# A planner's look-ahead limit for the MLP's second sweep, and the centering of two inner norms on ScalarE, in a one-layer decoder kernel

## The chip, the cores and the metric

The kernel runs on one core of a Trainium2 chip. The metric is device microseconds (us) of one execution; lower is better. A core has five engines that run their own instruction queues in order and wait for each other by semaphores: TensorE (PE in the profile; its weight loads are PEld), VectorE (DVE), ScalarE (ACT), GpSimd (POOL) and SyncE (SP, which here only issues DMAs).

## What is computed

One post-normalised decoder layer over 512 tokens of 1024 features, in float32: every sub-layer does h <- LayerNorm(ALPHA * h + f(h)).

```
h = layer_norm(x, ln_in_g, ln_in_b)
h = layer_norm(ALPHA * h + hybrid_mixer(h, ...), ln_mix_g, ln_mix_b)   # three groups of heads, then h @ w_out
h = layer_norm(ALPHA * h + mem_attn(h, mem, ...), ln_mem_g, ln_mem_b)  # 4 heads over 256 memory tokens
u = relu(h @ w_up + b_up)                                              # 1024 -> 4096
h = layer_norm(ALPHA * h + (u * u) @ w_down + b_down, ln_ffn_g, ln_ffn_b)
```

The norms after the mixer and after the memory attention are called the two inner norms here ("mix" and "mem" in the names). Centering is the step (x - mean) * rs, rs being 1 / sqrt(variance + eps).

## The kernel before, in words

**Precision.** Matrix products are made in the fp32r type, with each operand split in two parts: hi = round(x), lo = x - hi, and three products hi*hi, hi*lo, lo*hi. So for every tile of weights or activations that enters a product there is a cast (hi) and a subtraction (lo). `two_parts` puts the cast on ScalarE and lets VectorE or GpSimd subtract; `split` lets the planner choose the engine of both.

**The planner.** The kernel's code does not issue instructions. It records operations in program order, each with an order number (`prio`, the value of `nc.clock`, which goes up by one with each operation), and at the end `nc.issue(LOOK)` places them one by one: of all operations whose inputs are placed it takes the one that can start first by its own table of prices, and of two with the same start the one with the lower number. The queue of every engine is the order of this placing. The front is the oldest operation that is not placed yet. An operation may be placed before its turn if its number lies at most `min(LOOK, op.ahead)` beyond the front's (line 300; LOOK is 560, `nc.ahead` is 1e9 except in one other stage), and if the buffers that it takes leave enough for all that comes before it in program order (`slots`, line 275).

**Buffers.** `pages` has 31 buffers of 128 x 1024 floats; the residual rows `res` (4), the transposed activations `h2T` (8), the kept MLP rows `keep` (16), and the split rows `a` (two for each step) are all pages. Raw weights (`wr`) have 4 buffers, split weights (`wh`, `wl`) 5 each. A buffer's new user waits for the last reader of the old one.

**The inner norms.** `gemm_tok` makes the 512 x 1024 output of `w_out` (or `w_mem_o`) in four tiles of 128 tokens, one after the other at its end. `after_mix` and `after_mem` are called for each tile: `residual` adds the two PSUM banks to `res[t]`, takes `bn_stats` and `bn_aggr` (mean, variance), `ve` = variance + eps on VectorE and `rs` = ve ** -0.5 on GpSimd; `center` then writes the centered rows in place (VectorE `tensor_scalar`). After every second tile `ln_transposed` transposes the rows on TensorE (`ps_lt`), applies gain and shift (`h`) and splits them into `h1T` or `h2T`, which the next stage's products (`ps_q`, `ps_up`) read. The products of the first 256 tokens can run while tiles 2 and 3 are still being normed.

**The MLP.** 4096 hidden features in 16 steps of 256. The first sweep does for step i two `up` products (`ps_up`, 24 matmuls each), keeps relu(.)^2 in `keep[i]`, and two steps later `first_products(i - 2)`: sums and differences of row blocks and weight blocks, split in `ends`, `mid`, `h_dn`, `l_dn`, and 18 matmuls into six PSUM banks (`ps_dn`; a scheme with 7 products for 8). `first_products(13)`, `(14)` and `(15)` come after the last `up`. The weight sums that the second sweep needs go to DRAM (tile `t`) and come back as `r_t`. The second sweep does the four products that are left: `second_parts(i)` splits `keep[i]` into two pages `a` and loads and splits `r_t` and `r_dn` (8 operations), and 24 matmuls follow, so that one step takes 32 order numbers. The last TAIL = 4 steps have their `second_parts` called together as `rest`, take pages `b` for their weights, and are multiplied tile by tile, so that the final norm overlaps them.

Of the kernel before, what the change touches and what calls it, by code (L numbers as in the profile page):

```python
# [12 lines left out]
AF = mybir.ActivationFunctionType  # L13
OP = mybir.AluOpType
# [350 lines left out]
def trunk_kernel(ctx: ExitStack, tc: tile.TileContext, x, mem, ln_in_g, ln_in_b, w_in, gate_w2,  # L365
# [23 lines left out]
    nc = Program(real)  # L389
    slack = [0.0]  # L390

    def page(shape, dtype, name):
        return pages.tile([128] + shape, dtype, name)
# [7 lines left out]
    def bank(name, shape=(512,)):  # L401
        return psum.tile([128] + list(shape), F32, name)
# [115 lines left out]
    def center(y, mv, rs):  # L518
        nc.vector.tensor_scalar(y, y, mv[:, 0:1], rs, op0=OP.subtract, op1=OP.mult)
# [174 lines left out]
    for j in range(1, NT):  # L694
# [3 lines left out]
        for h in range(IDX_H):  # L698
# [7 lines left out]
            else:  # L706
                nc.vector.scalar_tensor_tensor(acc[:, :n], r[:, :n], iw[:, j, h:h + 1], acc[:, :n],
                                               op0=OP.mult, op1=OP.add)
# [406 lines left out]
    def residual(res, t, parts, name):  # L1115

        n = 512 if len(parts) == 2 else 256
        st = small.tile([128, D // n, 6], F32, "st_" + name)
        for cc, o in parts:
            nc.vector.tensor_tensor(res[t][:, cc], o, res[t][:, cc], op=OP.add)  # L1120
            for c0 in range(cc.start, cc.stop, n):
                nc.vector.bn_stats(st[:, c0 // n, :], res[t][:, c0:c0 + n])
        return mean_scale(st, name)

    def normed(res, t, parts, name):

        mv, rs = residual(res, t, parts, name)
        center(res[t], mv, rs)

    def gain_shift(hat, gb, t, later=0.0):  # L1130
        nc.clock += later
# [6 lines left out]
    res = []  # L1138
# [8 lines left out]
    def after_mix(t, parts):  # L1147
        normed(res, t, parts, "mix")
        if t % 2:
            ln_transposed(res, *gb_cols["mix"], h1T, t - 1, 2)  # L1150
# [47 lines left out]
    def after_mem(t, parts):  # L1198
        normed(res, t, parts, "mem")
        if t % 2:  # L1200
            ln_transposed(res, *gb_cols["mem"], h2T, t - 1, 2)
# [30 lines left out]
    def two_parts(hi, lo, src):  # L1232
        nc.scalar.copy(hi, src)
        any_tt(lo, src, f32(hi), OP.subtract)

    def raw_down(i, k):
        r = wr_pool.tile([128, 1024], F32, f"r_dn{k}")
        nc.sync.dma_start(r, w_down[256 * i + 128 * k:256 * i + 128 * k + 128, :])
        return r
# [5 lines left out]
    def products(banks, todo, p, start, stop):  # L1245

        tt = slice(128 * p, 128 * p + 128)
        for name, (ah, al), (bh, bl) in todo:
            mm3(banks[name, p], ah[:, tt], al[:, tt], bh, bl, start, stop)
# [69 lines left out]
    def second_parts(i, tail):  # L1319

        a = [page([4, 256], F32R, f"a{n}") for n in range(2)]
        two_parts(a[0], a[1], keep[i])
        r0 = wr_pool.tile([128, 1024], F32, "r_t13")
        nc.sync.dma_start(r0, sums[i])
        r1 = raw_down(i, 1)
        right = []
        for r in (r0, r1):
            if tail:
                hi, lo = (page([1024], F32R, f"b{n}") for n in range(2))
            else:  # L1330
                hi, lo = wh_pool.tile([128, 1024], F32R, "h_dn"), wl_pool.tile([128, 1024], F32R, "l_dn")
            two_parts(hi, lo, r)
            right += [(hi[:, L], lo[:, L]), (hi[:, R], lo[:, R])]
        left = [(a[0][:, n, :], a[1][:, n, :]) for n in range(4)]
        return [("7", left[0], right[1]), ("5", left[1], right[0]), ("3", left[3], right[3]), ("2", left[2], right[2])]

    for i in range(NP - TAIL):
        todo = second_parts(i, False)
        if i == 0:
            for name, *_ in todo:  # L1340
                for p in range(2):
                    banks[name, p] = bank(f"ps_dn{name}")
        for one in todo:
            for p in range(2):
                products(banks, [one], p, i == 0, False)
    rest = [second_parts(i, True) for i in range(NP - TAIL, NP)]

# [12 lines left out]
    for p in range(2):  # L1360
        for n, name in enumerate(("7", "5", "3", "2")):
            for i, todo in enumerate(rest):
                products(banks, [todo[n]], p, False, i == TAIL - 1)
            if name == "7":
# [27 lines left out]
M_SLACK = 600.0  # L1392
DOWN_LATER = 60.0
TAIL = 4

_INS = ["x", "mem", "ln_in_g", "ln_in_b", "w_in", "gla_gate_w2", "gla_gate_b", "gla_norm_g", "dsa_w_uv",
        "w_out", "ln_mix_g", "ln_mix_b", "w_mem_q", "w_mem_kv", "w_mem_o", "ln_mem_g", "ln_mem_b",
# [19 lines left out]
```

## Time and profile before

| | |
|---|---|
| three runs of the kernel | 821.04, 821.12, 822.54 us; median 821.12 us |
| the execution that was profiled | 822.55 us, of which 820.8 us are the span from the first instruction to the last |
| busy share of the span | PE 96%, PEld 81%, DVE 78%, ACT 40%, POOL 18% |
| granted TensorE clock, mean | 0.99 |

The rows below come from the trace of that one execution. Times are us from the span's start, durations us, "mean" ns. `[4.17 <-PE ps_up L356]` behind an instruction says that its engine sat idle for 4.17 us ahead of it and which instruction ended that. Every recorded operation has line 356, the planner's issuing line, so rows are told apart by the names of their tiles.

### The profile page before, as it was taken

Reading aid. Unit: us, or ns where it says so; the run is one execution under the profiler, and the core shown is the slowest. Engines: PE = TensorE matmul, PEld = TensorE weight load, DVE = VectorE, ACT = ScalarE, POOL = GpSimd, SP = SyncE. Lnnn points to the kernel's source line nnn. Section 1 sums busy time; section 2 is a strip of 40 time slices with the busy share of each in tenths; the row PEclk is TensorE's granted clock in tenths of the full one; section 3 lists DMA queues with packets and bytes.
Section 4 is the critical chain, followed back from the end, with each engine's and each line's share of the span. In section 5 each row is a group of like instructions: output and inputs, shape, how many; then the busy total and the mean of one; then the engine's idle time right before and its main releaser. Section 6 shows DMA issues by size and latency. Waiting matters only on the chain.

```text
span 820.8 us, 11293 instructions
## 1 busy us (share of the span) xinstructions
PE 790.4 (96%) x4177; PEld 662.5 (81%) x4177; DVE 636.3 (78%) x1118; ACT 328.0 (40%) x631; POOL 144.5 (18%) x169
## 2 busy tenths in 40 slices
PE   7999999999999999999999989999999999899995
PEld 5998768777877888899788888888888888678884
DVE  7737999997649984776953778997777776798778
ACT  5506634577535540244340233223323332585430
POOL 5320141354622210120530120000000000110001
PEclk8999999999999999999999999999999999999998
DMA  8520331603244535041322025466546555467632
GB/s 232 145 54 15 100 94 27 180 9 102 70 139 162 159 139 155 27 127 54 129 77 78 26 78 164 133 216 201 184 148 211 202 167 170 147 214 243 195 126 103
DMA packets 99927, 106.70 MB, mean 130 GB/s; under 512 B 10448, under 2 KB 79136, under 8 KB 99872
## 3 DMA queue, kind: packets, MB, share of 16 engines
q1 hardware_dynamic: 97344, 99.00, 38.5%
q10 hardware_dynamic: 2528, 6.98, 2.5%
q8 instruction: 33, 0.54, 0.3%
q14 instruction: 22, 0.18, 0.1%
HBM read 94.69 MB, written 10.49 MB: 128 GB/s over the span
## 4 chain that ended last, share of the span: by engine, by line
PE 69%; DVE 16%; issue 3%; ACT 1%; POOL 1%; DVEq 0%; ACTq 0%; POOLq 0%
PE ps_up L356 21%; PE ps_dn L356 18%; PE ps_wo L356 5%; PE ps_wmo L356 4%; PE ps_q L356 4%; DVE acc L356 2%; DVE m L356 2%; PE ps_km L356 2%; DVE res L356 2%; PE ps_z L356 2%; PE ps_vm L356 2%; PE ps_dq L356 1%; DVE s L356 1%; PE ps_mo L356 1%; PE ps_ms L356 1%
## 5 line engine op out<-in xcount | busy, mean ns | idle before, releaser
L356 PE MATMUL ps_up<-h2T,h_up 128*128 128x512 f32 (+1 forms) x576 | 163.1, 368 | 0.4 <-POOL h2T L356 0.4
L356 PEld LDWEIGHTS ps_up<-h2T,h_up 128*128 128x128 f32 x576 | 105.4, 191 | 18.2 <-POOL h2T L356 0.6
L356 PE MATMUL ps_up<-h2T,l_up 128*128 128x512 f32 (+1 forms) x288 | 105.9, 368 | 0.0
L356 ACT ACTIVATE ur<-ps_up,gb_all 128x512 f32<-128x512 f32 x32 | 22.1, 690 | 103.6 <-PE ps_up L356 103.4
L356 PEld LDWEIGHTS ps_up<-h2T,l_up 128*128 128x128 f32 x288 | 55.0, 191 | 8.6
L356 PE MATMUL ps_dn<-h_dn,a 128*128 128x512 f32 x192 | 59.2, 389 | 0.0
L356 DVE TENSOR_TENSOR l_dn<-r_dn,h_dn 128x1024 fp32r<-128x1024 f32 (+1 forms) x44 | 45.2, 1027 | 4.9 <-ACT h_dn L356 3.5
L356 PE MATMUL ps_dn<-h_dn,ends 128*128 128x512 f32 x128 | 47.0, 390 | 0.7 <-DVE ends L356 0.7
L356 POOL TENSOR_TENSOR a<-keep,a 128x1024 fp32r<-128x1024 f32 x1 | 4.9, 4924 | 229.9 <-DVE l_dn L356 229.9
L356 PE MATMUL ps_q<-h1T,h_wmq 128*128 128x256 f32 (+1 forms) x192 | 44.7, 323 | 0.3 <-POOL h1T L356 0.3
L356 PEld LDWEIGHTS ps_dn<-h_dn,a 128*128 128x128 f32 x192 | 36.0, 188 | 7.4
L356 ACT ACTIVATE h<-ps_lt,gb_all 128x256 f32<-128x256 f32 x18 | 9.1, 566 | 80.3 <-PE ps_lt L356 80.3
L356 PE MATMUL ps_wmo<-h_wmo,oT 128*128 128x512 f32 x128 | 40.8, 393 | 0.0
L356 PE MATMUL ps_wo<-h_wo,mix 128*128 128x512 f32 x128 | 40.3, 392 | 0.0
L356 DVE TENSOR_TENSOR l_up<-r_up,h_up 128x1024 fp32r<-128x1024 f32 x31 | 37.8, 1223 | 1.9 <-ACT h_up L356 0.5
L356 PE MATMUL ps_dn<-l_dn,a 128*128 128x512 f32 x96 | 37.3, 389 | 0.0
L356 PEld LDWEIGHTS ps_q<-h1T,h_wmq 128*128 128x128 f32 x192 | 32.0, 190 | 2.8 <-POOL h1T L356 0.6
L356 DVE TENSOR_SCALAR h_up<-r_up 128x1024 fp32r<-128x1024 f32 x19 | 13.1, 692 | 22.7 <-PE ps_up L356 16.4
L356 PE MATMUL ps_q<-h1T,l_wmq 128*128 128x256 f32 (+1 forms) x96 | 30.7, 320 | 0.0
L356 PEld LDWEIGHTS ps_dn<-h_dn,ends 128*128 128x128 f32 x128 | 24.0, 188 | 6.1 <-DVE ends L356 1.2
L356 PEld LDWEIGHTS ps_wo<-h_wo,mix 128*128 128x128 f32 x128 | 24.0, 188 | 4.9
L356 PEld LDWEIGHTS ps_wmo<-h_wmo,oT 128*128 128x128 f32 x128 | 24.0, 188 | 4.8
(407 smaller groups left out, 2085.2 us busy)
## 6 DMA issues: line engine op xcount, KB each, us to landing
r_dn<-in_w_down_dram SPq DMA_DIRECT2D x48, 512.0 KB, 4.3
r_up<-in_w_up_dram SPq DMA_DIRECT2D x32, 512.0 KB, 4.2
r_t<-t SPq DMA_DIRECT2D x16, 512.0 KB, 4.1
r_kvv<-in_w_mem_kv_dram SPq DMA_DIRECT2D x8, 512.0 KB, 4.3
r_kvk<-in_w_mem_kv_dram SPq DMA_DIRECT2D x8, 512.0 KB, 3.6
r_wo<-in_w_out_dram SPq DMA_DIRECT2D x8, 512.0 KB, 4.6
r_wmq<-in_w_mem_q_dram SPq DMA_DIRECT2D x8, 512.0 KB, 5.2
r_wmo<-in_w_mem_o_dram SPq DMA_DIRECT2D x8, 512.0 KB, 3.2
```

The lines of the kernel that those rows point to most:

```text
L356: f(*[real(a) for a in args], **{k: real(a) for k, a in kwargs.items()})
```

## The change

Two edits. The centering of the two inner norms is done by ScalarE: VectorE makes a one-column tile off = -mean * rs, and ScalarE computes rs * x + off over the 1024 columns, in place. And the operations of `second_parts` for the first twelve steps of the second sweep get a look-ahead limit of 120 order numbers in place of 560; their products and the four steps of `rest` keep 560.

```
     def normed(res, t, parts, name):

         mv, rs = residual(res, t, parts, name)
-        center(res[t], mv, rs)
+        off = tiny(1, "off_" + name)
+        nc.vector.tensor_scalar(off, mv[:, 0:1], rs, -1.0, op0=OP.mult, op1=OP.mult)
+        nc.scalar.activation(res[t], res[t], AF.Identity, bias=off, scale=rs)
...
     for i in range(NP - TAIL):
+        nc.ahead = SECOND_AHEAD
         todo = second_parts(i, False)
+        nc.ahead = 1e9
...
+SECOND_AHEAD = 120.0
```

Since the planner places all operations together, both edits can change the order of any queue after them.

## Rows read from the trace of the kernel before

**Rows 1.** The page: span, and busy time of each engine with its share.

```profile
span 820.8 us, 11293 instructions
PE 790.4 (96%) x4177; PEld 662.5 (81%) x4177; DVE 636.3 (78%) x1118; ACT 328.0 (40%) x631; POOL 144.5 (18%) x169
```

**Rows 2.** The chain that ended last, in the MLP's first sweep (start, us, what).

```profile
515.99 10.88 PE ps_up L356 x48
526.87 4.08 PE ps_dn L356 x18
```

**Rows 3.** Windows: PE, PEld, DVE, ACT, POOL busy (count), clock, DMA share, GB/s.

```profile
476.20:479.50 3.30, 3.30 (x18) 3.30 (x17) 3.07 (x4) 0.00 (x0) 1.49 (x1) 0.50 0.66 189
...
706.20:724.40 18.20, 13.53 (x56) 9.92 (x55) 18.17 (x31) 9.80 (x16) 5.06 (x2) 1.00 0.59 193
724.40:789.40 65.00, 65.00 (x288) 53.87 (x287) 53.82 (x51) 38.98 (x39) 1.17 (x1) 1.00 0.70 225
```

**Rows 4.** Timeline where the memory attention passes into the MLP (start, us, engine).

```profile
469.95 2.94 ACT L356 CAST h_up<-r_up 128x1024 fp32r<-128x1024 f32 x3 [2.62 <-PE ps_wmo L356]
...
471.58 2.37 POOL L356 TENSOR_TENSOR l_up<-r_up,h_up 128x1024 fp32r<-128x1024 f32 x1
471.65 2.85 DVE L356 TENSOR_SCALAR res<-res,mv_mem,rs_mem 128x1024 f32<-128x1024 f32 x1 [0.67 <-POOL rs_mem L356]
471.75 0.40 PE L356 MATMUL ps_up<-h2T,h_up 128*128 128x256 f32 x2
...
474.64 0.63 PE L356 MATMUL ps_lt<-ident,res 128*128 128x128 f32 x4 [2.03 <-DVE res L356]
...
482.11 1.47 PE L356 MATMUL ps_lt<-ident,res 128*128 128x128 f32 x12
```

**Rows 5.** Timeline where the mixer passes into the memory attention: PE, then DVE.

```profile
350.20 0.40 PE L356 MATMUL ps_q<-h1T,h_wmq 128*128 128x256 f32 x2
...
357.38 1.47 PE L356 MATMUL ps_lt<-ident,res 128*128 128x128 f32 x12
...
360.03 0.62 PE L356 MATMUL ps_q<-h1T,h_wmq 128*128 128x256 f32 x3 [0.35 <-POOL h1T L356]
...
350.20 0.81 DVE L356 TENSOR_SCALAR res<-res,mv_mix,rs_mix 128x1024 f32<-128x1024 f32 x1 [0.67 <-POOL rs_mix L356]
```

**Rows 6.** Groups by shape (busy, mean ns), then tiles (min/median/max ns).

```profile
L356 ACT CAST h_up<-r_up 128x1024 fp32r<-128x1024 f32 x13 | 13.5, 1055 | 21.9 <-PE ps_dn L356 19.3 <-PE ps_wmo L356 2.6
L356 ACT ACTIVATE h<-ps_lt,gb_all 128x256 f32<-128x256 f32 x18 | 9.1, 566 | 80.3 <-PE ps_lt L356 80.3
L356 ACT CAST h2T<-h 128x256 fp32r<-128x256 f32 x10 | 3.5, 417 | 0.0
...
L356 DVE TENSOR_SCALAR res<-res,mv_mem,rs_mem x4: 807/814/2849, 456.3 to 478.5; 128x1024 f32<-128x1024 f32 x4
L356 DVE TENSOR_SCALAR ve_mem<-mv_mem x4: 136/154/154, 455.4 to 476.1; 128x1 f32<-128x1 f32 x4
```

**Rows 7.** Timeline, opening of the kernel: POOL and DVE.

```profile
8.07 1.44 POOL L356 TENSOR_TENSOR rs_in<-ve_in,mhalf 128x1 f32<-128x1 f32 x2 [2.87 <-DVE ve_in L356]
...
8.21 0.16 DVE L356 TENSOR_SCALAR ve_in<-mv_in 128x1 f32<-128x1 f32 x1
```

**Rows 8.** Timeline between the MLP's two sweeps: DVE, POOL, PE.

```profile
701.66 1.23 DVE L356 TENSOR_TENSOR a<-keep,a 128x1024 fp32r<-128x1024 f32 x1 [4.17 <-PE ps_up L356]
...
717.28 2.51 DVE L356 TENSOR_TENSOR keep<-keep,s 128x256 f32<-128x256 f32 x1
...
714.58 4.92 POOL L356 TENSOR_TENSOR a<-keep,a 128x1024 fp32r<-128x1024 f32 x1 [229.87 <-DVE l_dn L356]
...
720.98 0.50 PE L356 MATMUL ps_dn<-l_dn,mid 128*128 128x512 f32 x1 [1.65 <-DVE l_dn L356]
```

**Rows 9.** Tiles `a` and `keep` (min/median/max ns, first and last start us).

```profile
L356 ACT CAST a<-keep x16: 1042/1050/1062, 637.5 to 746.1; 128x1024 fp32r<-128x1024 f32 x16
...
L356 DVE TENSOR_TENSOR keep<-keep,s x16: 416/421/2507, 495.3 to 717.3; 128x256 f32<-128x256 f32 x16
```

## The prediction

> **What bounds the kernel now.** I read the page first: TensorE is busy for 96% of the span, VectorE for 78%, ScalarE for 40% [rows 1]. So an edit can gain only where TensorE stands still or is slowed. The chain of waits shows how regular the rest is: in the MLP's first sweep it consists of runs of 48 `ps_up` and 18 `ps_dn` matmuls without a gap [rows 2], at 10.88 / 48 = 0.227 us for a matmul. Nothing can be won there. The windows, stage by stage, then show two places near the change where TensorE loses time.
>
> The first is the passage from the memory attention to the MLP. The timeline shows TensorE waiting 2.03 us, up to 474.64, for the centered rows of the third tile; their centering on VectorE took 2.85 us while GpSimd ran a `l_up` subtraction of 2.37 us [rows 4], against a median of 0.81 us [rows 6]. After this wait the granted clock is 0.50, which is 1.2 GHz, for 3.30 us [rows 3]: another 1.65 us lost, 3.7 us in all. The passage from the mixer to the memory attention has the same work without the stall: there the centering took 0.81 us, and from TensorE's first product to the twelve transposes of the last tile pass 357.38 - 350.20 = 7.2 us [rows 5], against 482.11 - 471.75 = 10.4 us here [rows 4]. The difference, 3.2 us, is the better price of the stall, since it is what the twin does not pay.
>
> The second is the junction of the sweeps, 706.20 to 724.40. TensorE does the products of `first_products(13)`, `(14)` and `(15)` there, 54 matmuls, which at 0.227 us take 12.2 us; the window lasts 18.2 us, so 6.0 us are lost. VectorE is busy for 18.17 of the 18.2 us [rows 3], so it is the bound. Yet it had idled 4.17 us right before, up to 701.66, at the head of its queue an `a` subtraction of the second sweep that waited for `up` matmuls [rows 8]. By the code the two share no data; what `a` waits for there is a page, one that the last `up` products still read as `h2T`. Behind it on VectorE's queue stood the weight sums of `first_products(14)`. Later GpSimd runs another `a` subtraction for 4.92 us [rows 8], and a `keep` subtraction of VectorE that takes 0.42 us in the median takes 2.51 us beside it [rows 8, 9].
>
> **The change part by part: the limit.** Order numbers from the code: if `second_parts(0)` begins at S, then `first_products(13)` begins at S - 130, `up(31)` at S - 159, `up(30)` at S - 188. With 560 ahead, the first `a` was allowed from about S - 560, some four and a half first-sweep steps (96 numbers each) before `first_products(13)`: at 15 us a step, 10.88 + 4.08 [rows 2], that is about 639 us, and the first cast stands at 637.5 [rows 9]. With 120 it is allowed ten operations into `first_products(13)`, which the front cannot pass before the end of `up(31)` at 706.2. So `a(0)` can no longer stand in VectorE's queue at 701.66. What leaves VectorE's queue ahead of the late matmul at 720.98 is then the wait of 4.17, the subtraction of 1.23, and 2.51 - 0.42 = 2.09 beside GpSimd: 7.5 us, more than the 6.0 us that can be won. Against this: the rows of `rest` keep the old limit. `second_parts(12)` begins at S + 384 and is allowed 560 before that, at S - 176, twelve operations into `up(30)`, or about 697 us. Its rows can fill the same hole. They find two free pages (31, less 8 `h2T`, 4 `res`, 16 `keep` and one `ends`), so they need not wait for `h2T`, but two subtractions, 2.5 us, come back: 5.0 us. And `first_products(15)` needs relu, square and its own chain of small operations after `up(31)`; I take 1 us off for it. **Junction: -4.0 us**, with 0 (the hole stays) and -6.0 as ends.
>
> In the second sweep TensorE is full, 65.00 of 65.00 us, VectorE has 53.82 and ScalarE 38.98 [rows 3]. The limit moves casts from before 746 to later; ScalarE's idle 40% hides them. 120 numbers are 3.75 steps of 24 matmuls, some 20 us, and the loads were held to two steps before by the four `wr` buffers, so SP's queue is hardly changed. Cost: 0; without that cover see the fourth rival.
>
> **The centering.** Removed from VectorE: 8 operations of 0.81. Added: 8 `off`, like `ve` one column, 0.15, and on ScalarE 8 passes over 1024 columns. Such a pass isn't in the trace; a cast of that size takes 1.055, and a 256-column pass with scale and bias from tiles 0.566 against 0.417 for a plain cast [rows 6], so 1.055 + 0.15 = 1.20 us. Bounds: 1.055, and 1.055 + 4 x 0.15 = 1.65 if the extra grew with the columns; I take 1.20, the nearest difference as it stands. With under 0.1 for one hand-over more (the whole detour over GpSimd for `rs` is a wait of 0.67 [rows 5]) the chain of a tile grows by 0.15 + 0.1 + 0.39 = 0.64 us, and VectorE gets 0.66 us back.
>
> Tiles 0 and 1 at both passages are hidden: two more tiles of 24 matmuls, 48 x 0.227 = 10.9 us, follow on TensorE. For tiles 2 and 3 the cover is the next stage's product over the first 256 tokens, and at the mixer's end it just runs out: TensorE waits 0.35 us for `h1T` [rows 5]. There the longer chain shows, less what VectorE gives back: 0 to +0.64, **mixer passage: +0.3 us**. At the MLP's passage the stall goes, because ScalarE's centering stands neither behind GpSimd nor in front of VectorE's next tile; but ScalarE has three casts of `h_up` from 469.95 to 472.89 [rows 4]. The centering is ready at 471.65 + 0.25 = 471.9, as the third cast begins. If it comes behind, it ends at 474.1 and the wait shrinks by 0.4 only, unless the planner has given TensorE products to do before the transposes, which it does when it knows of the delay. Ends: -0.4 and -3.7. I take the twin's 3.2 less 0.6 for the longer chain: **MLP passage: -2.6 us**.
>
> [...]
>
> **Sum.** -4.0 + 0.3 - 2.6 = -6.3 us. Against the profiled execution that is 822.55 - 6.3 = 816.25 (span 814.5 and the same 1.75 around it); that execution is 1.43 above the median of the three, and against the median, which I forecast, it is 821.12 - 6.3 = 814.8 us.
>
> **The rivals.** 1. Only the junction pays: the centering queues behind the third cast, -0.4 + 0.3 - 4.0, 817.0 us. For it: the cast starts within 0.1 us of the centering. Against it: both passages are planned anew.
> 2. `off` is held by GpSimd: it ends at 474.1, the centering at 475.4, TensorE waits 2.9 instead of 2.03; 821.12 - 4.0 + 0.3 + 0.9 = 818.3. Against it: a one-column `tensor_scalar` ran in its usual 0.16 us from 8.21, inside GpSimd's `rs_in` that began at 8.07 [rows 7]. For it: that GpSimd operation has one column too. [...]
> 3. The limit doesn't do what it says, since `rest` is free of it: its rows take the pages and the hole, and the junction loses 6.0 us still. 821.12 + 0.3 - 2.6 = 818.8.
> 4. The second sweep starves, and it gets slower. `rest` may take the 7 pages that are free at its start (31, less 4 `res`, 2 gains, 16 `keep`, 2 `a`) while steps 4 to 11 may not. Then `a` of the next step gets its page only as the last is released, and TensorE waits for a cast of 1.05 and a subtraction of 1.23 in every step: 2.3 us. It is slower than before from (6.3 + 1.6) / 2.3, four such steps; with six of them 821.12 - 6.3 + 13.8 = 828.6. For it: the code's limits. Against it: of two operations that can start together the planner takes the earlier number, and pages get free with every step.
> 5. Neither place pays and nothing is lost, because other orders bring other stalls: 821.1.
>
> **How the numbers follow.** A measurement of this kernel tells about 0.2%, 1.6 us, from no change. Chances: forecast 0.44 (own range 811.4 to 817, from the ends -6.0 and -3.7 to about half the gain), rival 1 0.15, rival 2 0.05, rival 3 0.12, rival 5 0.13, rival 4 0.11. Faster: 0.44 + 0.15 + 0.05 + 0.12 = 0.76; same 0.13; slower 0.11. The range runs from 811.4 (both stalls gone whole) to 821.0, which leaves out rival 4, half of rival 5 and little below.
>
> **What would show it.** Right: no wait of TensorE on centered rows near 472, clock 1.00 in the 12 us after, the twelve transposes some 8 us behind the first `ps_up`; VectorE without an idle stretch between 697 and 702, no `a` on GpSimd, and about 14 us between the last `ps_up` and the first second-sweep matmul; the second sweep still at 0.227 us. Centerings of 1.2 us on ScalarE. Wrong: transposes waiting for ScalarE, `a` of steps 12 and up ahead of `first_products(14)` on a page of `h2T`, or waits on `a` within the second sweep.

## The result and the profile after

The kernel after takes 812.34 us (median of 4 runs, 812.27 to 812.93), the kernel before, run beside it, 821.63 us (821.04 to 822.54). The ratio is 0.9888, 95% interval 0.9874 to 0.9903: 9.3 us or 1.1% faster. Forecast were 814.8 us and a gain of 6.3 us. The direction and the two places were right; both were sized too small, and the mixer passage, where a small loss was forecast, gained a little.

The first lines of the page of the profiled execution after (812.93 us), which answer to [rows 1]: span, and busy time of each engine with its share and count.

```profile
span 811.2 us, 11285 instructions
...
PE 788.2 (97%) x4177; PEld 661.9 (82%) x4177; DVE 630.8 (78%) x1127; ACT 335.1 (41%) x635; POOL 140.2 (17%) x164
```

TensorE did the same 4177 matmuls in nearly the same busy time; the span is 9.6 us shorter. To see where, I took the start of the first or last matmul of each stage from the tiles' rows of both traces; each number is the time from one such start to the next.

| from ... to | before | after |
|---|---|---|
| start ... first `ps_wo` (opening, mixer) | 304.8 | 305.5 |
| ... first `ps_q` (mixer's output) | 45.4 | 45.4 |
| ... first `ps_wmo` (mixer passage, memory attention) | 72.5 | 72.1 |
| ... first `ps_up` (memory's output) | 49.0 | 49.0 |
| ... first `ps_dn` (MLP passage) | 40.0 | 36.0 |
| ... last `ps_up` (first sweep) | 194.3 | 194.3 |
| ... first `ps_dn` on an `a` (junction) | 18.4 | 12.5 |
| ... last `ps_dn` (second sweep) | 86.8 | 86.8 |
| ... end | 9.6 | 9.6 |

The MLP passage gave 4.0 us, the junction 5.9, the mixer passage 0.4. The opening is 0.7 longer. No operation of the change lies in it, and in the profiled executions below the first `ps_wo` starts anywhere from 304.4 to 305.4 us (305.4 in `a0_on_pool`, too, which has neither edit), so I take this for spread.

The windows after (us; PE, PEld, DVE, ACT, POOL busy with counts, clock, DMA share, GB/s), answering to [rows 3]: MLP passage, last `up` products, junction, second sweep.

```profile
472.20:508.20 36.00, 35.90 (x257) 33.80 (x257) 31.08 (x57) 17.37 (x28) 2.51 (x3) 1.00 0.42 134
691.80:702.68 10.88, 10.88 (x50) 9.01 (x49) 9.39 (x14) 4.76 (x7) 0.00 (x0) 1.00 0.43 147
702.68:715.00 12.32, 12.32 (x57) 10.18 (x56) 12.29 (x21) 10.83 (x15) 3.02 (x1) 1.00 0.72 234
715.00:780.00 65.00, 65.00 (x288) 53.85 (x287) 53.52 (x50) 39.98 (x40) 2.42 (x2) 1.00 0.69 223
```

TensorE is busy 35.90 of 36.00 us in the passage, at full clock (1.00, which is 2.4 GHz), and 12.32 of 12.32 in the junction, which is about what 54 matmuls at 0.227 us need (12.3): TensorE has next to no wait left at either place. VectorE is still full in the junction (12.29 of 12.32), but TensorE no longer waits for it.

The timeline after at the MLP passage (start, us, engine, instruction, idle time before it and what ended it), answering to [rows 4].

```profile
472.84 1.06 POOL L356 TENSOR_SCALAR h_up<-r_up 128x1024 fp32r<-128x1024 f32 x1
472.90 0.21 DVE L356 TENSOR_SCALAR off_mem<-mv_mem,rs_mem 128x1 f32<-128x1 f32 x1
...
473.15 1.24 ACT L356 ACTIVATE res<-res,off_mem,rs_mem 128x1024 f32<-128x1024 f32 x1 [5.14 <-DVE off_mem L356]
...
474.06 0.68 DVE L356 TENSOR_SCALAR h_up<-r_up 128x1024 fp32r<-128x1024 f32 x1
474.23 0.93 POOL L356 TENSOR_TENSOR rs_mem<-ve_mem,mhalf 128x1 f32<-128x1 f32 x1 [0.33 <-DVE ve_mem L356]
474.30 1.03 ACT L356 CAST h_up<-r_up 128x1024 fp32r<-128x1024 f32 x1
474.53 0.60 PE L356 MATMUL ps_lt<-ident,res 128*128 128x128 f32 x4
...
476.04 1.25 ACT L356 ACTIVATE res<-res,off_mem,rs_mem 128x1024 f32<-128x1024 f32 x1 [0.71 <-DVE off_mem L356]
477.47 1.47 PE L356 MATMUL ps_lt<-ident,res 128*128 128x128 f32 x12
```

The transposes of the third and fourth tile stand without a wait; the third tile's centering ends at 474.39, 0.14 us before TensorE comes to it. The three `h_up` casts that stood together on ScalarE are spread: GpSimd has one, VectorE one, ScalarE one, between the two centerings.

The timeline after at the junction, answering to [rows 8].

```profile
693.82 0.69 DVE L356 TENSOR_TENSOR r_dn<-r_dn 128x512 f32<-128x512 f32 x1
...
697.05 0.69 DVE L356 TENSOR_SCALAR h_dn<-r_dn 128x1024 fp32r<-128x1024 f32 x1 [1.09 <-PE ps_up L356]
697.85 1.23 DVE L356 TENSOR_TENSOR l_dn<-r_dn,h_dn 128x1024 fp32r<-128x1024 f32 x1
...
700.25 1.22 DVE L356 TENSOR_TENSOR a<-keep,a 128x1024 fp32r<-128x1024 f32 x1
...
702.05 1.22 DVE L356 TENSOR_TENSOR a<-keep,a 128x1024 fp32r<-128x1024 f32 x1
```

The weight sums `r_dn` of `first_products(14)` begin at 693.82, 8.9 us before the last `up` product ends at 702.68. Before, they stood behind the waiting `a` of [rows 8] and began at 702.81, 3.4 us before 706.20:

```profile
702.81 0.69 DVE L356 TENSOR_TENSOR r_dn<-r_dn 128x512 f32<-128x512 f32 x1
```

So they come 5.5 us earlier, measured from the end of the `up` products: the wait of 4.17 and the subtraction of 1.23 [rows 8]. The two `a` rows that do come early, at 700.25 and 702.05, stand behind `l_dn`. They belong to `rest`: with the limit on `rest` too they are gone (`rest_limited` below).

Tiles after (min/median/max ns, first and last start): the new operations, and `a` ([rows 6, 9]).

```profile
L356 DVE TENSOR_SCALAR off_mem<-mv_mem,rs_mem x4: 205/213/215, 456.6 to 475.8; 128x1 f32<-128x1 f32 x4
L356 ACT ACTIVATE res<-res,off_mem,rs_mem x4: 1244/1245/1248, 456.8 to 476.0; 128x1024 f32<-128x1024 f32 x4
...
L356 ACT CAST a<-keep x16: 1037/1048/1054, 699.0 to 751.3; 128x1024 fp32r<-128x1024 f32 x16
L356 DVE TENSOR_TENSOR a<-keep,a x15: 1211/1217/1219, 700.2 to 758.0; 128x1024 fp32r<-128x1024 f32 x15
L356 POOL TENSOR_TENSOR a<-keep,a x1: 2419/2419/2419, 715.0 to 715.0; 128x1024 fp32r<-128x1024 f32 x1
```

### The profile page after: what moved, and what is told of

It is laid out like the page before. It is cut to its first block, busy times and chain, and to the rows that moved or that the text cites. A ratio compares the mean times of both kernels' runs of the same rounds, so it can differ in the third digit from the quotient of the medians.

```text
span 811.2 us, 11285 instructions
## 1 busy us (share of the span) xinstructions
PE 788.2 (97%) x4177; PEld 661.9 (82%) x4177; DVE 630.8 (78%) x1127; ACT 335.1 (41%) x635; POOL 140.2 (17%) x164
## 4 chain that ended last, share of the span: by engine, by line
PE 76%; DVE 10%; issue 2%; ACT 1%; POOL 0%; DVEq 0%; ACTq 0%; POOLq 0%
PE ps_up L356 22%; PE ps_dn L356 19%; PE ps_wmo L356 5%; PE ps_wo L356 5%; PE ps_q L356 4%; PE ps_z L356 2%; PE ps_km L356 2%; PE ps_vm L356 2%; PE ps_gg L356 1%; DVE res L356 1%; PE ps_dq L356 1%; DVE acc L356 1%; PE ps_mo L356 1%; DVE s L356 1%; PE ps_o L356 1%
## 5 line engine op out<-in xcount | busy, mean ns | idle before, releaser
L356 PE MATMUL ps_up<-h2T,h_up 128*128 128x512 f32 (+1 forms) x576 | 161.3, 366 | 0.1
L356 POOL TENSOR_TENSOR l_dn<-r_dn,h_dn 128x1024 fp32r<-128x1024 f32 x1 | 3.1, 3071 | 236.8 <-ACT h_dn L356 236.8
L356 DVE MAX8 m<-acc 128x8 f32<-128x256 f32 (+2 forms) x48 | 25.9, 550 | 0.3
```

Of the source, the lines that this page charges most:

```text
L356: f(*[real(a) for a in args], **{k: real(a) for k, a in kwargs.items()})
```

## The experiments

Medians of the kernel before beside them were 821.41 us (first four), 821.13 us (second four) and 821.46 us (last four). The ratios and their 95% intervals are to those runs; they are taken over all runs, so they are not exactly the quotients of the medians. "Stage" lengths are those of the table above.

### Each half alone: `limit_only` and `centre_only`

The two halves of the diff, each by itself:

```
-        center(res[t], mv, rs)                             # centre_only
+        off = tiny(1, "off_" + name)
+        nc.vector.tensor_scalar(off, mv[:, 0:1], rs, -1.0, op0=OP.mult, op1=OP.mult)
+        nc.scalar.activation(res[t], res[t], AF.Identity, bias=off, scale=rs)
...
+        nc.ahead = SECOND_AHEAD                            # limit_only
         todo = second_parts(i, False)
+        nc.ahead = 1e9
```

> The limit without the ScalarE centering. Theory (the two stalls are separate, and the limit undoes only the one between the sweeps): 6.0 us below the kernel before, about 815.6 us; first ps_dn of the second sweep some 6 us earlier behind the last ps_up, the 2.03 us wait on centered rows and the half clock after it still there. Rival (the gain comes from the new order as a whole, each edit needs the other): less than 4 us.

Measured: 816.15 us, ratio 0.9934 (0.9917 to 0.9950). Junction 12.5 us as after, MLP passage 40.0 as before: a gain of 5.3, near the 5.9 of the junction. The rest went in the second sweep, 87.7 in place of 86.8. The timeline has there one wait of TensorE for an `a`:

```profile
731.27 1.20 PE L356 MATMUL ps_dn<-h_dn,a 128*128 128x512 f32 x4 [0.57 <-DVE a L356]
```

It is not the fourth rival, which has `a` waiting for a page: VectorE was busy for all of the 6 us from 726 to 732 and had other subtractions ahead of this `a` in its queue.

> The ScalarE centering without the limit. Theory: the passage from the memory attention to the MLP gives 4.1 us, the passage from the mixer nothing, the junction stays at 18.2 us: about 817.5 us. Rival (the centering pays at both inner norms, since it frees VectorE): more than 5 us, or, if the longer chain is paid at the mixer's passage, 3 us or less.

Measured: 818.37 us, ratio 0.9964 (0.9951 to 0.9977). The MLP passage is 36.0, the junction 20.0. The waits of TensorE at the junction add up to 4.7 us, as before; the extra 1.6 us are the clock, as the windows of this execution show (same columns as above; 0.75 and 0.59 are means over windows that hold stretches at 1.2 and at 2.4 GHz).

```profile
716.00:719.60 3.60, 3.40 (x11) 2.64 (x12) 3.60 (x7) 2.48 (x3) 0.11 (x1) 0.75 0.58 166
719.60:721.60 2.00, 2.00 (x7) 1.56 (x6) 0.59 (x2) 1.45 (x3) 1.17 (x1) 0.59 0.55 217
```

The two halves gain 5.3 + 3.0 = 8.3 us alone and about 9.2 together, and each is shown to work at its own place.

### What the limit acts on: `rows_limited`, `loads_limited`, `step0_free`, `ahead240`

All four have the new centering. `rows_limited` and `loads_limited` split the limit within `second_parts`:

```
     a = [page([4, 256], F32R, f"a{n}") for n in range(2)]
+    nc.ahead = 1e9 if tail else SECOND_AHEAD      # rows_limited: around this call alone
     two_parts(a[0], a[1], keep[i])
+    nc.ahead = 1e9                                # loads_limited: limit from here to the return
     r0 = wr_pool.tile([128, 1024], F32, "r_t13")
```

In both, the two lines of the change around the call of `second_parts` are taken out.

> The changed kernel with the limit on the rows alone (cast and subtraction of a), the loads and splits of r_t and r_dn free to come 560 ahead. Theory (an early row on a page is what blocks VectorE): as the changed kernel, 812.3 us. Rival (early weights fill the raw-weight buffers and hold up first_products(15)): between 814 and 818.3 us.

> The opposite: the changed kernel with the limit on the loads and splits of r_t and r_dn alone, the rows a free. Theory (rows): the 4.2 us hole of VectorE ahead of first_products(14) and the 6.0 us between the sweeps are back, 818.3 us. Rival (weights): 812.3 us.

Measured: `rows_limited` 812.19 us, 0.9887 (0.9873 to 0.9902), junction 12.5; `loads_limited` 817.92 us, 0.9960 (0.9945 to 0.9974), junction 18.4 with the same four waits of TensorE as before (0.75, 1.87, 0.39 and 1.64 us). The limit works through the rows alone.

`step0_free` lets one step out of it:

```
-        nc.ahead = SECOND_AHEAD
+        nc.ahead = SECOND_AHEAD if i > 0 else 1e9
```

> The kernel after, but the limit leaves out the first step of the second sweep, whose rows may then be taken as early as in the kernel before. If one low part of those rows in VectorE's queue, waiting for a page of SBUF, makes the whole stall at the junction, its 6 us come back: about 818 us. If the stall needs the rows of several steps, or GpSimd's rows, it stays near 812 to 813 us.

Measured: 817.35 us, 0.9951 (0.9935 to 0.9967): 5.0 us above the kernel after, junction 18.5. In its timeline the one row stands at the same place in VectorE's queue as before, with the same wait, and TensorE waits for what is queued behind it.

```profile
697.06 1.23 DVE L356 TENSOR_TENSOR a<-keep,a 128x1024 fp32r<-128x1024 f32 x1 [4.17 <-PE ps_up L356]
...
702.99 0.49 PE L356 MATMUL ps_dn<-h_dn,ends 128*128 128x512 f32 x1 [0.75 <-DVE ends L356]
...
705.37 0.80 PE L356 MATMUL ps_dn<-h_dn,mid 128*128 128x512 f32 x1 [1.89 <-ACT mid L356]
```

These waits are 2.6 us. The other 3.4 us are the clock: it was 0.76 from 702 to 707 us and 0.56 from 707 to 712, which loses 1.2 and 2.2 us. So it is chance that the junction is as long as before, where the clock was full. The row of step 0 alone is shown to cost its waits, and not the whole 6 us; the profiled execution was also the slowest of the four (818.67 us, the fastest 816.14).

`ahead240` has `SECOND_AHEAD = 240.0`.

> The kernel after with the limit at 240 instead of 120: in VectorE's queue the rows of the first four steps come early, yet still behind the weights of the last products but one. If only a row that stands ahead of those weights on a page of h2T makes the stall, the junction stays at 12.5 us and the time at 812 to 813 us. If early rows as such fill VectorE at the junction, 1 to 6 us come back: 813 to 818 us.

Measured: 812.37 us, 0.9888 (0.9873 to 0.9902), junction 12.6. Its trace has three `a` subtractions before 704 us, one more than the kernel after, all behind `l_dn`:

```profile
700.13 1.22 DVE L356 TENSOR_TENSOR a<-keep,a 128x1024 fp32r<-128x1024 f32 x1
...
702.00 1.22 DVE L356 TENSOR_TENSOR a<-keep,a 128x1024 fp32r<-128x1024 f32 x1
...
703.47 1.22 DVE L356 TENSOR_TENSOR a<-keep,a 128x1024 fp32r<-128x1024 f32 x1
```

Rows that come early behind the weights of `first_products(14)` cost nothing. It is their place in VectorE's queue that counts, not how many they are; more than three early rows were not seen.

### Who shares the junction's loss: `no_pool_a` and `a0_on_pool`

Both are the kernel before with one line of `second_parts` changed: no low part of `a` on GpSimd, or only that of step 0, and always.

```
-        two_parts(a[0], a[1], keep[i])
+        nc.scalar.copy(a[0], keep[i])
+        nc.vector.tensor_tensor(a[1], keep[i], f32(a[0]), op=OP.subtract)            # no_pool_a
+        (pool_tt if i == 0 else any_tt)(a[1], keep[i], f32(a[0]), OP.subtract)       # a0_on_pool
```

> The kernel before, but no low part of second-sweep rows is formed by GpSimd, whose 4.92 us subtraction stood beside VectorE's 2.51 us sum of keep at the junction. If GpSimd's subtraction cost the last 2 us of the junction, it falls from 18.4 to about 16.4 us and the time to about 819.5 us. If the row waiting in VectorE's queue made all 6 us, the junction stays at 18 us or more and the time at 820 to 823 us.

Measured: 819.99 us, 0.9986 (0.9977 to 0.9996), junction 17.2. The sum of `keep` that took 2.51 us beside GpSimd takes 0.42:

```profile
715.46 0.42 DVE L356 TENSOR_TENSOR keep<-keep,s 128x256 f32<-128x256 f32 x1
```

Before, TensorE had four waits at the junction, 4.7 us in all: the 1.65 of [rows 8], and ahead of it these three.

```profile
707.59 0.49 PE L356 MATMUL ps_dn<-h_dn,ends 128*128 128x512 f32 x1 [0.75 <-DVE ends L356]
709.97 0.50 PE L356 MATMUL ps_dn<-h_dn,mid 128*128 128x512 f32 x1 [1.89 <-ACT mid L356]
...
712.01 0.50 PE L356 MATMUL ps_dn<-h_dn,mid 128*128 128x512 f32 x1 [0.39 <-DVE mid L356]
```

Only the first two are left in `no_pool_a`, the same two as in `step0_free`. So two sources are shown: 2.6 us behind the `a` row that waits in VectorE's queue, 1.65 us beside GpSimd's `a`. The wait of 0.39 is not GpSimd's, since it ended at 712.01, before that subtraction began at 714.58. VectorE had a second `a` subtraction just ahead of that `mid`, at 710.40; it has one there in `no_pool_a` too, but TensorE, at a lower clock, came later. The other 1.2 us of the 5.9 lie in the matmuls next to the waits, which take 0.33 us and more from start to start in place of 0.227.

That the junction fell by only 1.2 us is the clock of the profiled execution: 0.91 from 704 to 709 us and 0.75 from 709 to 714, 1.7 us lost.

> The kernel before, but the low part of the first second-sweep rows is put on GpSimd, so that no such row stands in VectorE's queue ahead of the last products. If the wait in VectorE's queue was the cause, most of the 6 us of the junction go, about 815 to 817 us, and the stall in the MLP passage stays. If GpSimd's weights for the up products then wait behind that row, PE stalls on them instead, and the time is near 821 us or above.

Measured: 820.42 us, 0.9986 (0.9977 to 0.9995). A miss: the row left VectorE's queue, and most of the loss came back in another form.

```profile
700.88 3.23 POOL L356 TENSOR_TENSOR a<-keep,a 128x1024 fp32r<-128x1024 f32 x1 [217.09 <-ACT ur L356]
...
702.07 3.42 DVE L356 TENSOR_TENSOR ends<-keep,ends 128x512 fp32r<-128x512 f32 x2 [0.22 <-ACT ends L356]
...
704.14 0.62 ACT L356 CAST ends<-keep 128x512 fp32r<-128x512 f32 x1 [2.10 <-POOL a L356]
```

The two `ends` sums take 3.42 us beside GpSimd's subtraction, against 1.29 before (the same pair, at 706.85), and ScalarE's next cast waits 2.10 us for GpSimd. From the last `up` to the last `ps_dn` it takes 103.7 us, against 105.2 before and 99.3 after (here the two parts of that time can't be split, since matmuls on `a` were put among the first products). Of the 4.4 us above the kernel after, 2.0 are a wait of TensorE for `mid` at 709.49, and 1.65 the clock behind it, 0.50 from 709.9 to 713.2.

### Why the centering took 2.85 us: `no_pool_up`

The kernel before, but `split` gives the low part of the up weights to VectorE always (`up` sets the flag).

```
+        if no_pool[0]:
+            nc.vector.tensor_tensor(lo, src, f32(hi), op=OP.subtract)
+            return
```

> The kernel before, but the low part of the up weights is never formed by GpSimd. It asks why VectorE's centering of the last tile of memory attention took 1.64 us before the MLP's first transposes, against 0.81 us for others. If a GpSimd subtraction beside it held it, the centering falls to about 0.8 us, the transposes come earlier, and part of the stall of 4.1 us in the MLP passage goes: 1 to 4 us, so 817 to 820 us. If the stall comes from VectorE's queue alone, the passage stays at 40.0 us and the time at 820 to 822 us. The junction between the sweeps should stay at 18.4 us, 6 us of it lost, in both.

The 1.64 us named there is a slip: the centering in question is the 2.85 us of [rows 4], that of the third tile.

Measured: 818.89 us, 0.9969 (0.9960 to 0.9979), MLP passage 36.5. Without a GpSimd subtraction beside it the same centering takes 0.81 us, and the wait of 2.03 us [rows 4] is gone:

```profile
471.52 0.81 DVE L356 TENSOR_SCALAR res<-res,mv_mem,rs_mem 128x1024 f32<-128x1024 f32 x1 [0.66 <-POOL rs_mem L356]
...
472.48 0.63 PE L356 MATMUL ps_lt<-ident,res 128*128 128x128 f32 x4
```

The cause of the stall is shown: GpSimd's `l_up`, not VectorE's queue. The junction is 18.4 again, but by chance: its waits are 3.3 us in place of 4.7, and the clock, 0.50 from 707.1 to 710.5, took 1.7. That the new centering removes the same stall is a second way to the same end: VectorE need not touch those 1024 columns.

### Which passage pays: `mem_only`

The kernel after, with the mixer's norm on VectorE as before.

```
+        if name == "mix":
+            center(res[t], mv, rs)
+            return
```

> The kernel after, with the mixer's norm centered on VectorE as before and only the memory's on ScalarE. If the mixer's passage lost nothing and won nothing, its stages take 45.4 and 72.1 to 72.5 us and the time is 812 to 813 us. If ScalarE's centering costs the mixer's passage its 0.3 us of the prediction, this version is 0.3 us faster; if the 0.4 us by which the memory attention became shorter come from it, it is 0.4 us slower.

Measured: 812.53 us, 0.9898 (0.9876 to 0.9920); the kernel after is not told apart from it. The stage from `ps_q` to `ps_wmo` is 72.5 us again, with the wait of 0.35 us on `h1T` that [rows 5] show; so the 0.4 us by which it became shorter come from the mixer's new centering.

### Too late, or all of them late: `ahead16` and `rest_limited`

The limit at 16, and the limit of 120 on the last four steps too.

```
-SECOND_AHEAD = 120.0
+SECOND_AHEAD = 16.0                                        # ahead16
...
+    nc.ahead = SECOND_AHEAD                                # rest_limited
     rest = [second_parts(i, True) for i in range(NP - TAIL, NP)]
+    nc.ahead = 1e9
```

> The kernel after with the limit at 16 instead of 120, so rows of the second sweep come later still. If rows taken too late starve the second sweep (the prediction's fourth rival), waits of TensorE on a appear in it, 1 to 2.3 us for each step hit, and the second sweep takes 88 to 95 us instead of 86.8: 814 to 820 us. If the idle time of ScalarE and VectorE there covers it, nothing changes: 812 to 813 us.

Measured: 817.28 us, 0.9947 (0.9932 to 0.9961): 4.9 us above the kernel after. The junction is 14.5, the second sweep 90.6. Starvation is real, though not by the path of the fourth rival, the pages of `a`: the loads of the weights are limited too, ScalarE waits for them, and TensorE for their splits. Of the 3.8 us by which the second sweep is longer, 1.7 are the clock, 0.51 from 716.0 to 719.4 in the profiled execution.

```profile
715.92 3.68 PE L356 MATMUL ps_dn<-h_dn,a 128*128 128x512 f32 x8 [1.89 <-ACT h_dn L356]
...
721.32 1.05 ACT L356 CAST h_dn<-r_t 128x1024 fp32r<-128x1024 f32 x1 [2.61 <-DMA r_t<-t]
...
725.47 0.50 PE L356 MATMUL ps_dn<-l_dn,a 128*128 128x512 f32 x1 [1.32 <-DVE l_dn L356]
```

> The kernel after, with the limit on the last four steps of the second sweep too, whose rows stand early in the queues of the kernel after. If these rows cost something at the junction or in the second sweep, the time falls by up to 1 us, to about 811.5 us; if they are harmless, as the trace of after suggests, it stays at 812 to 813 us.

Measured: 813.08 us, 0.9893 (0.9879 to 0.9908), not told apart from the kernel after. The early rows of `rest` cost nothing; without them (its first `a` subtraction stands at 704.83) the junction is rather longer, 13.4, with one wait:

```profile
711.78 0.50 PE L356 MATMUL ps_dn<-h_dn,mid 128*128 128x512 f32 x1 [0.66 <-ACT mid L356]
```

None of the twelve is faster than the kernel after by more than the runs can tell; `rows_limited`, `ahead240`, `mem_only` and `rest_limited` are not told apart from it.

## Why the prediction was right, and where its sizes were off

**Junction, -4.0 forecast, -5.9 measured.** The mechanism holds step by step: an `a` of step 0 that waits at the head of VectorE's queue, the weights behind it, GpSimd's `a` beside the `keep` sum. `step0_free` and `no_pool_a` show the first and the last. That the wait is for a page of `h2T` follows from the code, as the trace shows only that `up` matmuls ended it. The mis-sized step is what was taken off: "two subtractions, 2.5 us, come back", and "1 us off" for the chain of `first_products(15)`. The two subtractions came (700.25 and 702.05), but behind the weights and not ahead of them. In the 10.88 us of the last `up` products VectorE had been busy 6.5 us before and is 9.4 after; they use time that was idle. The chain of `first_products(15)` shows no wait of TensorE. The term was the end of its range, -6.0, and the time from the last `ps_up` to the first matmul on an `a` 12.5 us, not about 14. Against the sign that was named, one `a` is still GpSimd's, but at 715.00, when TensorE is past the junction.

**MLP passage, -2.6 forecast, -4.0 measured.** The mis-sized step is the price by "the twin's 3.2 less 0.6 for the longer chain". The 0.6 is nothing: the chain is longer, with 1.245 us for the centering (forecast 1.20) and 0.21 for `off` (0.15), but TensorE has products of the first 256 tokens until it is done. The twelve transposes come 477.47 - 472.01 = 5.5 us behind the first `ps_up`, where about 8 were forecast and the twin had 7.2. And the twin's 3.2 was too low a price: gone are the wait of 2.03, the 1.65 of the clock [rows 3], and a wait of 0.35 for `h2T`, together 4.0.

**Mixer passage, +0.3 forecast, -0.4 measured.** The same error: the chain was priced on the path, but the transposes came 356.44 - 350.86 = 5.6 us behind the first `ps_q`, in place of 7.2, and the wait of 0.35 for `h1T` [rows 5] went.

**Second sweep, 0 forecast, 0 measured.** 65.00 of 65.00 us busy, as before.

**The sum.** -4.0 - 5.9 - 0.4 + 0.7 for the opening is the 9.6 us of the two spans. The profiled execution of before held a loss that not every execution has, the 1.65 us of the clock. Without it, and without the opening, the stages give 8.7; the runs of before that lie lowest, at about 820.9, against 812.3 after, give 8.6. So taking 1.43 off, to come from that execution to the median of 821.12, fits, though the clock was not traced in the runs at that median. But then the sum takes the clock off twice: the price of the MLP passage has it in it, and the median of 821.12 does not hold it. In `no_pool_a` and `a0_on_pool`, where the clock stayed at 1.00 after the same wait, the passage took 38.5 us, 2.5 more than after. Against that median the -2.6 is nearly right, by luck: what the price left out and what it counted twice cancel. What separates 814.8 from 812.3 is then the junction (1.9) and the mixer passage (0.7).

**The rivals.** The first, centering behind the third cast, did not come: the casts were spread over three engines. The second, `off` held until `l_up` ends (in [rows 4] 471.58 + 2.37 = 473.95, and 0.15 for `off` itself), fell: `off` started at 472.90 inside a GpSimd pass from 472.84 to 473.90, and took 0.21 us. Of the eight `off`, two ran beside such a pass, this one and the one at 351.88; both took 0.212 us, the other six 0.205 to 0.215. The Trainium skill, "SBUF — State Buffer", section "Who interferes with whom", says that a `tensor_scalar` *can* enter a mode that takes VectorE's second pair of ports, which it shares with GpSimd, and that whoever issues first then has the pair for the whole instruction. On 1024 columns the runs agree (2.85 us beside `l_up`, 0.81 without, in `no_pool_up`); one column was not held, and why not, no run here shows. The same section of the Trainium skill says that ScalarE waits for no one. The two centerings that ran beside GpSimd agree, at 1242 and 1244 ns against 1244 to 1248 for the other six. The third rival's order came true in part: rows of `rest` come early, but behind the weights, and cost nothing. The fourth did not come at 120, nor by its own path at 16. The fifth is out.

## What to carry to other kernels

In an in-order queue, look for the instruction that waits for a buffer and not for data: what it costs is the work queued behind it, and delaying that one instruction by a limit is free as long as its own deadline is far (here free at 120, and 4.9 us at 16). A stall that a twin stage does not have can be worth more than the twin's difference, as here: price the wait, the clock that falls after it, and the smaller waits that follow, each from its row, and ask whether the time that you subtract from holds the clock's part. Before two junctions of the same length are called the same, look at the clock in both: here it made up the length by chance in two experiments. A longer chain costs nothing while the engine that waits at its end has other work that may be placed first; ask for that work before a price is put on the chain.

## What the runs showed of the hardware that was not expected

**The clock after a short wait.** The same wait of 2.0 us for `res` at the MLP passage was followed by a lower granted clock in some profiled executions (before, `limit_only`) and not in others (`no_pool_a`, `a0_on_pool`). The windows of 474 to 477 and 477 to 480 us in `limit_only`, where 0.71 and 0.72 are means of stretches at 1.2 and at 2.4 GHz, and then in `no_pool_a`:

```profile
474.00:477.00 3.00, 2.52 (x15) 2.55 (x16) 2.90 (x6) 0.00 (x0) 0.83 (x1) 0.71 0.60 176
477.00:480.00 3.00, 3.00 (x21) 3.00 (x20) 2.10 (x3) 0.00 (x0) 0.66 (x1) 0.72 0.64 193
```

```profile
474.00:477.00 3.00, 2.68 (x23) 2.71 (x24) 2.90 (x6) 0.00 (x0) 0.98 (x1) 1.00 0.59 174
477.00:480.00 3.00, 3.00 (x27) 3.00 (x27) 1.95 (x3) 0.00 (x0) 0.51 (x1) 1.00 0.56 183
```

The passage took 40.0 us in the first and 38.5 in the second. At the junction `centre_only` and `loads_limited` have the same four waits; in the first the clock fell behind the last of them and the junction took 20.0 us, in the second it stayed at 1.00 and the junction took 18.4. It also fell there in `step0_free`, `no_pool_a`, `no_pool_up` and `a0_on_pool`, and not in before. The 25 runs of before beside the second four experiments lie in two groups, 13 from 820.57 to 821.13 and 10 from 822.23 to 822.53 us, with two between, 1.5 us apart. Their mean granted clocks are 0.991 to 0.993 in the lower group and 0.989 to 0.991 in the upper, which fits the clock as the reason; where in the run it fell was not traced for them. The 4 runs of after, with neither stall, lie within 0.66 us.

**A one-column VectorE operation beside GpSimd** takes its usual time (`off`, 0.21 us), but GpSimd's own one-column `rs_mem` took 0.93 us where it began inside a 1024-column VectorE pass (474.06 to 474.74), and 1.49 in before where it began inside VectorE's `l_up` subtraction, against 0.55 for the tile ahead of it, which began inside a VectorE sum with one operand in PSUM.
